# A float32 transformer block on one core: gate and up with another order of products, subtractions from PSUM, and down's low parts on GpSimd

## The chip, the cores and the metric

One core of a Trainium2 chip runs the whole program. Its engines are TensorE (PE in the profile; PEld are its weight loads), VectorE (DVE), ScalarE (ACT), GpSimd (POOL) and SyncE (SP), which here issues nearly all DMAs. The metric is the device time of one launch in microseconds (us), the median of several runs. "Faster" and "slower" are told against the kernel before.

## What is computed

The reference is one layer of a decoder with 512 tokens and model width 2048, all in float32: mixing (attention and convolution) with an output projection, then a feed-forward network. The change is in the second half:

```
h2 = _rms_norm(x, norm2_g)
x = x + (silu(h2 @ w_gate) * (h2 @ w_up)) @ w_down      # w_gate, w_up: 2048 x 5632, w_down: 5632 x 2048
```

The norm's factor is one number per token, so the kernel multiplies without it and puts it on the results: silu(r * gate) * (r * up).

## The kernel before

**Three products for one.** A float32 operand is split into a high part (the value rounded to the float32r format) and a low part (the rest), and each product is three matmuls: high x high, high x low, low x high (lines 1181, 1183, 1184 for gate and up; 1421 to 1423 for down). Each matmul here has 512 columns.

**Seven products for eight.** Gate, up and down each use Winograd's form of Strassen's scheme: 2 x 2 blocks take seven block products, numbered by `ORDER` (7, 1, 4, 2, 5, 6, 3) and, for down, `D_ORDER`, at the price of sums of blocks. The token side's sums are made once and stay in 56 slots as high and low halves (`ops`, seven products x eight pieces). The weights' sums are made while they stream in, by GpSimd (`plus`, line 172), in place in eight raw buffers.

**Steps.** I call half a product a step: one unit of weights (`next_unit`, line 292), two banks, twelve matmuls. Seven products are 14 steps, a half; a block (`Up(n)`, n = 0 to 10) is two halves, 28 steps, and makes 512 columns of gate and up. Down has 12 rounds (`Down(t)`) of 14 steps. Each step takes the sums due (`sums_now`), runs what is due in the list `evacs`, splits the weights that are two steps ahead (`split_up_to`: two ScalarE copies, `near` in PSUM at line 268 and `hi` at 269, and VectorE's low part at 270), asks for up to two loads (`pump`, line 234), issues its matmuls, and then runs what is due in the list `extras`. `later(n, ...)` puts a call n runs of its list ahead.

**The order of the work is written out by hand**: each engine's instructions run in the order in which the program issues them, so an instruction that waits holds up all behind it on its engine, and on SyncE a DMA that waits holds up all DMAs behind it.

**What follows a product** (`Up.done`, line 1197) is done in the step after its last. Four sums are kept per block, called (i, k): here i = 0 is gate and i = 1 up, k is the token half, and each lies in two tiles (a = 0, 1). A sum is complete after its last product of the second half. A bank is copied to a tile (`keep`, line 1191: ScalarE for a = 0, VectorE for a = 1) or added to it (`add`, line 1195). A product whose matmuls begin without `start` adds onto the one that lies in its banks: product 4 onto 7, 2 onto 1, 3 onto 5. Products 1 and 6 go to tiles of their own, and GpSimd then takes these from or adds them to the others (ten instructions a block, line 1195).

**What follows a block**: ScalarE's silu with the norm's factor (`gate`, line 1243), VectorE's product of the two with the factor (`weigh`, line 1252), VectorE's transposes of 32 x 32 blocks (`turn`, line 1256), a store to DRAM (`store`, line 1261). Steps are counted from 0: the weigh of token half 0 falls in step 1 of the next block, that of half 1 in step 2, the turns a step later. Then two pairs (`Pair`) are read back, from steps 6 and 16 of the next block on, as tiles l and r; GpSimd sums them (lines 1143 to 1148), and `piece` makes down's seven operands of each: a ScalarE copy `near` to PSUM (line 1110), a ScalarE copy for the high part (line 1114), VectorE's low part (line 1115), and a store (`od`, line 1100).

Beside it, sums for down's end are turned: `turn_x2` reads four pieces (z) and `turn_x2_now` transposes them on VectorE (zt, line 1288), at steps 9 and 12, 25 and 27 of blocks 1 to 8. `norm2` sums the squares on TensorE after step 2 of block 0.

All these tiles come from one pool of 73 slots (`slot`, line 138).

## Time and profile before

| what | value |
|---|---|
| median of 3 runs | 1947.52 us (1946.16 to 1948.61) |
| the profiled execution: its own time | 1949.01 us |
| its span, first to last instruction | 1947.3 us |
| mean granted TensorE clock | 0.984 |
| TensorE busy (modelled ends) | 1877.9 us |
| VectorE, ScalarE, GpSimd busy | 1480.2, 1365.2, 1085.8 us |
| gate and up, by their matmuls | 582 to 1506 us |
| down, by its matmuls | 1506 to 1943 us |

In the profile, a group's row has line, engine, operation, what it writes and reads (buffer numbers left out), shape and count, then busy us and mean ns, then the engine's idle time just before these instructions and what ended it. A window's row has the stretch in us from the span's start, its length, and for each engine the busy time with the number of instructions, then the granted clock, the share of the DMA engines and GB/s. Matmuls overlap and their ends are modelled, so a busy TensorE isn't one at its full pace: the distance between starts is what counts.

### The profile page before, as it was taken

What the parts mean: (1) busy time and instruction counts of PE and PEld (TensorE: products, weight loads), DVE (VectorE), ACT (ScalarE), POOL (GpSimd) and SP (SyncE); (2) the same over time, 40 slices, a digit from 0 to 9 for tenths busy, and PEclk for the clock granted to TensorE, in tenths of its full rate; (3) what the DMA queues carried; (4) which work ended last, traced back from release to release, by engine and by line L of the source; (5) the groups of instructions that cost most, each with busy time, mean ns of one, the idle gap of its engine ahead of it and who ended that gap; (6) DMA issues with size and microseconds to landing.
All of it is one profiled execution on the core that took longest, in us unless ns stands there. A gap on an engine that the chain in (4) does not pass through costs nothing.

```text
span 1947.3 us, 26413 instructions
## 1 busy us (share of the span) xinstructions
PE 1877.9 (96%) x8370; PEld 1542.3 (79%) x8370; DVE 1480.2 (76%) x2147; ACT 1365.2 (70%) x1893; POOL 1085.8 (56%) x762
## 2 busy tenths in 40 slices
PE   9999999999999998989989898998999799999999
PEld 7888888888887786877878687776878688888887
DVE  6788878997786767777776777777677777777777
ACT  6356544543567787878878787887879587777776
POOL 0135532100016566667566676756667588878776
PEclk9999999999999999999999999999999999999999
DMA  7242343244343376677657676666659897567545
GB/s 269 86 136 82 100 123 100 82 136 141 135 133 89 109 189 178 178 188 185 180 160 185 173 187 178 192 176 161 178 168 294 257 308 265 179 214 244 174 154 117
DMA packets 382987, 330.35 MB, mean 170 GB/s; under 512 B 171648, under 2 KB 311552, under 8 KB 382848
## 3 DMA queue, kind: packets, MB, share of 16 engines
q1 hardware_dynamic: 382704, 328.66, 57.5%
q8 instruction: 66, 1.08, 0.2%
q14 instruction: 73, 0.60, 0.1%
q10 hardware_dynamic: 144, 0.01, 0.0%
HBM read 255.56 MB, written 64.63 MB: 164 GB/s over the span
## 4 chain that ended last, share of the span: by engine, by line
PE 79%; DVE 7%; DMA 4%; SPq 3%; ACT 2%; POOL 2%; issue 2%; DVEq 0%; POOLq 0%; ACTq 0%
PE out L1183 10%; PE out L1184 10%; PE out L1181 10%; PE out L1422 7%; PE out L1421 7%; PE out L1423 7%; PE o L305 3%; PE o L303 3%; PE o L304 3%; DVE wl L270 2%; PE cq L303 2%; PE cq L305 1%; PE cq L304 1%; SPq L1130 1%; ACT wh L269 1%
## 5 line engine op out<-in xcount | busy, mean ns | idle before, releaser
L1183 PE MATMUL out<-wl,h 128*128 128x512 f32 x1232 | 491.9, 399 | 40.0 <-DVE wl L270 39.6
L1181 PE MATMUL out<-wh,h 128*128 128x512 f32 x1232 | 488.9, 397 | 10.6 <-DVE b8c L1195 1.7
L1184 PE MATMUL out<-wh,h 128*128 128x512 f32 x1232 | 488.1, 396 | 0.0
L1183 PEld LDWEIGHTS out<-wl,h 128*128 128x128 f32 x1232 | 236.0, 192 | 100.7 <-DVE wl L270 51.5
L1181 PEld LDWEIGHTS out<-wh,h 128*128 128x128 f32 x1232 | 236.2, 192 | 66.4 <-issue 13.5
L1184 PEld LDWEIGHTS out<-wh,h 128*128 128x128 f32 x1232 | 236.4, 192 | 48.3
L1421 PE MATMUL out<-wh,a 128*128 128x512 f32 x620 | 243.0, 392 | 8.6 <-issue 5.2
L1422 PE MATMUL out<-wl,a 128*128 128x512 f32 x620 | 242.7, 392 | 1.8 <-DVE wl L270 1.8
L1423 PE MATMUL out<-wh,a 128*128 128x512 f32 x620 | 242.3, 391 | 0.0
L274 ACT CAST wh<-w 128x1024 fp32r<-128x1024 f32 (+2 forms) x94 | 96.8, 1031 | 152.4 <-PE o L304 64.8
L252 DVE TENSOR_TENSOR wl<-w,wh 128x1024 fp32r<-128x1024 f32 (+2 forms) x95 | 113.3, 1192 | 40.9 <-ACT wh L274 39.2
L1421 PEld LDWEIGHTS out<-wh,a 128*128 128x128 f32 x620 | 117.7, 190 | 33.5 <-issue 5.6
L1422 PEld LDWEIGHTS out<-wl,a 128*128 128x128 f32 x620 | 117.6, 190 | 27.2 <-DVE wl L270 3.0
L1423 PEld LDWEIGHTS out<-wh,a 128*128 128x128 f32 x620 | 117.5, 190 | 24.0
L1431 DVE TENSOR_TENSOR y<-y,out 128x512 f32<-128x512 f32 x164 | 105.9, 683 | 21.4 <-PE out L1423 19.8
L514 DVE SCALAR_TENSOR_TENSOR y<-bu,cst,y 128x511 f32<-128x511 f32 (+14 forms) x120 | 89.9, 750 | 0.7
L303 PE MATMUL o<-mh_c,wh 128*128 128x512 f32 x128 | 51.1, 399 | 0.0
L303 PE MATMUL cq<-hh,wh 128*128 128x512 f32 x128 | 50.6, 395 | 0.0
L305 PE MATMUL o<-mh_c,wl 128*128 128x512 f32 x128 | 50.0, 391 | 0.0
L304 PE MATMUL cq<-hl,wh 128*128 128x512 f32 x128 | 50.0, 390 | 0.0
L305 PE MATMUL cq<-hh,wl 128*128 128x512 f32 x128 | 50.0, 390 | 0.0
L304 PE MATMUL o<-ml_c,wh 128*128 128x512 f32 x128 | 50.0, 390 | 0.0
(2411 smaller groups left out, 4955.6 us busy)
## 6 DMA issues: line engine op xcount, KB each, us to landing
od<-a SPq DMA_DIRECT2D x154, 256.0 KB, 4.9
a<-od SPq DMA_DIRECT2D x154, 256.0 KB, 5.5
w<-in_wi SPq DMA_DIRECT2D x58, 512.0 KB, 3.3
w<-in_wo SPq DMA_DIRECT2D x32, 512.0 KB, 3.3
x<-in_xT SPq DMA_DIRECT2D x16, 256.0 KB, 6.9
xr<-in_xT SPq DMA_DIRECT2D x16, 256.0 KB, 3.6
x2d<-xr SPq DMA_DIRECT2D x16, 256.0 KB, 2.0
z<-x2d SPq DMA_DIRECT2D x64, 64.0 KB, 4.9
```

Source lines behind the costliest of these rows:

```text
L252: fn(*args)
L274: (nc.vector.tensor_copy if u == 0 else nc.scalar.copy)(hi[:, :n], t[:, :n])
L303: nc.tensor.matmul(out, wh, xh, start=start, stop=False)
L304: nc.tensor.matmul(out, wh, xl, start=False, stop=False)
L305: nc.tensor.matmul(out, wl, xh, start=False, stop=stop)
L1181: nc.tensor.matmul(b, x[:, high], wh[:, s], start=c == f == 0 and q in (7, 1, 5, 6), stop=False, skip_group_check=True)
L1183: nc.tensor.matmul(b, x[:, high], wl[:, s], start=False, stop=False, skip_group_check=True)
L1184: nc.tensor.matmul(b, x[:, low], wh[:, s], start=False, stop=c == f == 1, skip_group_check=True)
L1421: nc.tensor.matmul(b[:, lo:hi], x[:, high], wh[:, s], start=start, stop=False, skip_group_check=True)
L1422: nc.tensor.matmul(b[:, lo:hi], x[:, high], wl[:, s], start=False, stop=False, skip_group_check=True)
L1423: nc.tensor.matmul(b[:, lo:hi], x[:, low], wh[:, s], start=False, stop=last, skip_group_check=True)
L1431: getattr(eng, op)(t, t, src)
```

## The change

Gate and up take their products in the order 7, 1, 4, 6, 5, 2, 3. Product 6 now lies on 1 in its banks, and their sum is read from PSUM three times: kept or added for (0, 1), and taken from both gate sums by VectorE (`less`). GpSimd's ten instructions a block go. Up and gate change places (through the weights' addresses: i = 0 is up now, i = 1 gate). From block 1 on the norm's factor is put on up's sums where they are read from the bank (`scale` in `keep` and `add`); block 0, whose factor isn't there in time, scales in `weigh`. The product of the two is made by GpSimd. `piece` loses its copy to PSUM: GpSimd subtracts the high part from the value, two steps later (`rest`). A pair is summed nine steps after its first read and not four; z is read at steps 9 and 23 and turned seven steps later. The loads of a step are asked for ahead of its split, so after the extras of the step whose split frees their buffers. The sums 21 + 22 and 21 + 11 of the weights are due two and four steps sooner, and the buffers rotate otherwise. `norm2` comes a step later.

```diff
-ORDER = (7, 1, 4, 2, 5, 6, 3)
+ORDER = (7, 1, 4, 6, 5, 2, 3)
...
-                                up_block(n // 2 * 2, int(k[0]) - 1, int(k[1]) - 1, n % 2 * 4 + 2 * i)))
+                                up_block(n // 2 * 2, 2 - int(k[0]), int(k[1]) - 1, n % 2 * 4 + 2 * i)))
...
-            sums[base + 2 + i].append(plus(key["21"], key["21"], key["22"], 1024))
-            sums[base + 6 + i].append(plus(key["11"], key["21"], key["11"], 1024))
-            sums[base + 7 + i].append(plus(key["12"], key["11"], key["12"], 1024))
+            sums[base + i].append(plus(key["21"], key["21"], key["22"], 1024))
+            sums[base + 2 + i].append(plus(key["11"], key["21"], key["11"], 1024))
+            sums[base + 7 + i].append(plus(key["11"], key["11"], key["12"], 1024))
         works.extend((keys[c][k], last, "moves") for k, last in (
-            ("s", True), ("11", False), ("22", True), ("12", False), ("21", True), ("11", True), ("12", True)) for c in "AB")
-        bufs = {c: {"21": b["22"], "11": b["21"], "s": b["11"], "22": b["s"]} for c, b in bufs.items()}
+            ("s", True), ("11", False), ("22", True), ("11", False), ("21", True), ("12", True), ("11", True)) for c in "AB")
+        bufs = {c: {"21": b["22"], "11": b["21"], "s": b["s"], "22": b["11"]} for c, b in bufs.items()}
...
+        moves = works[u][2] == "moves"
+        if moves:
+            pump(RAW_BUFS, 2)
         lows_now()
         split_up_to(u + SPLIT_AHEAD)
-        if not lows:
-            pump(RAW_EARLY if u < 20 else RAW_BUFS, 2 if works[u][2] == "moves" else 99)
+        if not lows and not moves:
+            pump(RAW_EARLY if u < 20 else RAW_BUFS)
...
-    def piece(name, p, at, src):
-        n = src.shape[-1] // TH
-        near = psum["high"].tile([P, 1024], F32R, name=f"{name}n{at}", tag="h")[:, :n * TH]
-        nc.scalar.copy(near, src)
-        for k in range(n):
-            q, s = LAID[at + k], slice(k * TH, (k + 1) * TH)
+    def piece(p, at, src):
+        for k in range(src.shape[-1] // TH):
+            q, part = LAID[at + k], by_turns(src[:, k * TH:(k + 1) * TH])
             t = slot(f"a{q}_{p}", F32R)
-            nc.scalar.copy(by_tiles(t[:, :TH]), by_turns(src[:, s]))
-            nc.vector.tensor_sub(by_tiles(t[:, TH:]), by_turns(src[:, s]), by_turns(near[:, s].bitcast(F32)))
-            later(0, nc.sync.dma_start, od[p][:, (at + k) * T:(at + k + 1) * T], t.bitcast(F32), queue=extras)
+            nc.scalar.copy(by_tiles(t[:, :TH]), part)
+            later(1, rest, p, at + k, t, part)
+
+    def rest(p, at, t, part):
+        nc.gpsimd.tensor_sub(by_tiles(t[:, TH:]), part, by_tiles(t[:, :TH].bitcast(F32)))
+        later(1, nc.sync.dma_start, od[p][:, at * T:(at + 1) * T], t.bitcast(F32), queue=extras)
...
-            for at, fn in ((0, self.read_l), (1, self.read_r), (4, self.sums), (5, self.piece_r), (7, self.piece_l),
-                           (8, self.sum4), (9, self.piece_a), (11, self.piece_4)):
+            for at, fn in ((0, self.read_l), (2, self.read_r), (9, self.sums), (10, self.piece_r), (12, self.piece_l),
+                           (13, self.sum4), (14, self.piece_a), (16, self.piece_4)):
...
-                        nc.tensor.matmul(b, x[:, high], wh[:, s], start=c == f == 0 and q in (7, 1, 5, 6), stop=False,
+                        nc.tensor.matmul(b, x[:, high], wh[:, s], start=c == f == 0 and q in (7, 1, 5, 2), stop=False,
...
         def keep(self, i, k, a, b):
             t = self.c[i, k, a] = slot(f"b{self.n}c{i}{k}{a}")
-            (nc.vector.tensor_copy if a else nc.scalar.copy)(t, b)
+            if a == 0:
+                nc.scalar.activation(t, b, AF.Copy, scale=1.0 if i or not self.n else self.scale(k, a))
+            elif i or not self.n:
+                nc.vector.tensor_copy(t, b)
+            else:
+                nc.vector.tensor_scalar(t, b, self.scale(k, a), None, op0=ALU.mult)

-        def add(self, i, k, a, src, eng=nc.vector, op="tensor_add"):
-            t = self.c[i, k, a]
-            getattr(eng, op)(t, t, src)
+        def add(self, i, k, a, b):
+            t = self.c[i, k, a]
+            if i or not self.n:
+                nc.vector.tensor_add(t, t, b)
+            else:
+                nc.vector.scalar_tensor_tensor(t, b, self.scale(k, a), t, op0=ALU.mult, op1=ALU.add)
+
+        def less(self, k, a, b):
+            t = self.c[1, k, a]
+            nc.vector.tensor_sub(t, t, b)
...
                 elif q == 1:
-                    self.keep(2, 0, a, b)
+                    by(0, 0, a, b)
                 elif q == 4:
                     by(1, 0, a, b)
-                elif q == 2:
-                    by(0, 0, a, b)
+                elif q == 6:
+                    by(0, 1, a, b)
+                    self.less(0, a, b)
+                    self.less(1, a, b)
                 elif q == 5:
-                    self.add(1, 1, a, b, op="tensor_sub")
-                elif q == 6:
-                    self.add(2, 0, a, b)
+                    self.less(1, a, b)
                 else:
-                    self.add(0, 1, a, b)
...
+            if first:
+                return
+            if q in (6, 5):
+                later(1, self.gate, 6 - q, queue=extras)
+            elif q == 2:
+                self.dram = tc.dram_tile([T, T], F32, name=f"bd{self.n}")
+            if q in (2, 3):
+                later(0, self.weigh, q - 2)
+                later(2, self.turn, q - 2)
+                later(3, self.store, q - 2, queue=extras)
+            if q == 3:
+                for at in range(2):
+                    later(5 + 13 * at, Pair, self.dram, 2 * self.n + at, at, queue=extras)
...
         def weigh(self, k):
             for a in range(2):
-                t = self.c[1, k, a]
-                nc.vector.scalar_tensor_tensor(t, t, self.scale(k, a), self.c[0, k, a], op0=ALU.mult, op1=ALU.mult)
+                t = self.c[0, k, a]
+                if not self.n:
+                    nc.vector.tensor_scalar(t, t, self.scale(k, a), None, op0=ALU.mult)
+                nc.gpsimd.tensor_mul(t, t, self.c[1, k, a])
...
-                    if n == 0 and at_unit == 2:
+                    if n == 0 and at_unit == 3:
                         norm2()
-                    if 1 <= n <= 8 and at_unit in (9, 12, 25, 27):
-                        (turn_x2 if at_unit % 16 == 9 else turn_x2_now)(SUMS[2 * n - 2 + at_unit // 16])
+                    if 1 <= n <= 8 and at_unit in (9, 23):
+                        key = SUMS[2 * n - 2 + at_unit // 16]
+                        turn_x2(key)
+                        later(6, turn_x2_now, key)
```

More of the change, by code (lines that the diff above doesn't have):

```diff
@@ L1216, in done @@
-            if q == 6:
-                u = [self.c.pop((2, 0, a)) for a in range(2)]
-                for a in range(2):
-                    self.add(1, 0, a, u[a], nc.gpsimd, "tensor_sub")
-                for a in range(2):
-                    if first:
-                        self.c[0, 1, a] = u[a]
-                    else:
-                        self.add(0, 1, a, u[a], nc.gpsimd)
-                for a in range(2):
-                    self.add(1, 1, a, u[a], nc.gpsimd, "tensor_sub")
@@ L1227, in done @@
-            if not first and q in (2, 3):
-                k = q - 2
-                if k == 0:
-                    self.dram = tc.dram_tile([T, T], F32, name=f"bd{self.n}")
-                later(0, self.gate, k, queue=extras)
-                at = 1 if k else 6
-                later(at, self.weigh, k)
-                later(at + 1, self.turn, k)
-                later(at + 2, self.store, k, queue=extras)
-            if not first and q == 3:
-                later(5, Pair, self.dram, 2 * self.n, 0, queue=extras)
-                later(15, Pair, self.dram, 2 * self.n + 1, 1, queue=extras)
@@ L1240, in gate @@
-        def gate(self, k):
-            for a in range(2):
-                g = self.c[0, k, a]
-                nc.scalar.activation(g, g, AF.Silu, scale=self.scale(k, a))
+                    self.less(1, a, b)
+                else:
+                    self.add(0, q - 2, a, b)
+            if first:
[4 more added lines that the diff above has]
+                self.dram = tc.dram_tile([T, T], F32, name=f"bd{self.n}")
@@ L1247, in scale, with gate @@
             return n2["r"][:, i:i + 1]
+        def gate(self, k):
+            for a in range(2):
+                t = self.c[1, k, a]
+                nc.scalar.activation(t, t, AF.Silu, scale=self.scale(k, a))
         def weigh(self, k):
             for a in range(2):
-                t = self.c[1, k, a]
-                nc.vector.scalar_tensor_tensor(t, t, self.scale(k, a), self.c[0, k, a], op0=ALU.mult, op1=ALU.mult)
+                t = self.c[0, k, a]
+                if not self.n:
+                    nc.vector.tensor_scalar(t, t, self.scale(k, a), None, op0=ALU.mult)
+                nc.gpsimd.tensor_mul(t, t, self.c[1, k, a])
         def turn(self, k):
             for a in range(2):
-                nc.vector.transpose(self.c[0, k, a], self.c.pop((1, k, a)))
+                nc.vector.transpose(self.c[1, k, a], self.c.pop((0, k, a)))
         def store(self, k):
```

10 lines of the change are left out of this document (5 added, 5 removed).

## The prediction, made before the changed kernel was run

> **What bounds the kernel now.** I read the page first (its group rows are quoted where used), then the windows by stage, by block, and of one block's first steps.
>
> ```profile
> 804.94:817.86 12.92, 12.92 (x58) 1.00 0.47 104
> ...
> core 0: us, PE busy (x) PEld busy (x) DVE busy (x) ACT busy (x) POOL busy (x), PEclk, DMA share, GB/s
> 582.00:1506.00 924.00, 871.20 (x3703) 706.05 (x3702) 675.77 (x812) 737.96 (x942) 613.44 (x363) 0.97 0.65 176
> ...
> 663.00:742.00 79.00, 77.51 (x338) 1.00 0.62 164
> 827.00:911.50 84.50, 79.34 (x339) 0.98 0.70 184
> 911.50:997.00 85.50, 80.00 (x338) 0.96 0.66 179
> ...
> 1253.62:1275.43 21.81, 15.08 (x63) 11.31 (x62) 17.90 (x20) 14.13 (x18) 12.89 (x8) 1.00 0.51 146
> 1275.43:1338.83 63.40, 63.14 (x277) 51.40 (x275) 44.49 (x57) 53.46 (x71) 43.89 (x27) 1.00 0.72 189
> ```
>
> TensorE is the bound (busy 871 of 924 us in gate and up, more than any other engine); what a change can win is the time between its matmuls. Each row has the stretch, its length and, for each engine, busy time and instructions (the rows with one such pair are TensorE's alone). The first of them is a stretch without a wait: 57 intervals in 12.92 us, 0.2267 us a matmul. Twelve make one of my steps (half a product), 2.72 us; 28 steps make a block, 76.2 us. By that pace the 3703 matmuls of gate and up need 839.5 of 924.0 us: **84.5 us are lost**. Block 1 loses 79.0 - 338 x 0.2267 = 2.4, block 3 7.7, block 4 8.9. The last two rows cut block 8 behind its fifth step: the loss is all in the first five (63 matmuls need 14.3 of 21.8 us); the other 23 run clean (277 need 62.8 of 63.4).
>
> What fills VectorE there (its groups in block 8's first steps, but zt's of the whole run; then both engines' instructions in order of time):
>
> ```profile
> L1252 DVE SCALAR_TENSOR_TENSOR b7c<-b7c,n2r,b7c 128x512 f32<-128x512 f32 x4 | 6.5, 1658 | 0.0
> L1256 DVE STREAM_TRANSPOSE b7c<-b7c 128x512 f32<-128x512 f32 x4 | 2.6, 680 | 0.0
> L1288 DVE STREAM_TRANSPOSE zt<-z 128x512 f32<-128x512 f32 x16 | 11.3, 708 | 32.2 <-DMA z<-x2d 12.0 <-DMA w('12', 'u18A')_12598<-in_wgu 4.4 <-DMA w('12', 'u6A')_8068<-in_wgu 4.2
> L1115 DVE TENSOR_TENSOR a<-p13r,p13n 128x256 fp32r<-128x256 f32 x1 | 0.4, 382 | 0.0
> ...
> 1261.95 5.12 DVE L1252 SCALAR_TENSOR_TENSOR b7c<-b7c,n2r,b7c 128x512 f32<-128x512 f32 x2
> 1266.99 1.21 DVE L270 TENSOR_TENSOR wl<-w('11', 'u16B')_11690,wn 128x1024 fp32r<-128x1024 f32 x1
> ...
> 1261.36 2.38 POOL L172 TENSOR_TENSOR w('21', 'u16B')_11588<-w('21', 'u16B')_11588,w('22', 'u16B')_11801 128x1024 f32<-128x1024 f32 x1
> 1263.70 2.81 POOL L172 TENSOR_TENSOR w('11', 'u16A')_11663<-w('21', 'u16A')_11559,w('11', 'u16A')_11663 128x1024 f32<-128x1024 f32 x1
> ...
> L1183 PE MATMUL out<-wl,h 128*128 128x512 f32 x1232 | 491.9, 399 | 40.0 <-DVE wl L270 39.6
> ```
>
> VectorE is busy 17.9 us and idle 3.9, the whole 21.8 where five steps give 13.6; the idle time is before zt, whose read hasn't landed (32.2 us over the run). Two weigh instructions (L1252) take 5.1 us together while GpSimd adds weights; the weights' low part (L270) stands behind them, and TensorE's largest wait is for that (last row). So two things make the loss: the weigh that drags beside GpSimd, and the transpose queued before its read is there.
>
> **The change part by part.** Rows for the prices:
>
> ```profile
> L1195 DVE TENSOR_TENSOR b7c<-b7c,out x18: 673/680/690, 1203.0 to 1260.2; 128x512 f32<-128x512 f32 x18
> L1195 POOL TENSOR_TENSOR b7c<-b7c,b7c x10: 1280/1290/1302, 1211.8 to 1257.8; 128x512 f32<-128x512 f32 x10
> L1252 DVE SCALAR_TENSOR_TENSOR b7c<-b7c,n2r,b7c x4: 703/1538/2853, 1261.9 to 1270.0; 128x512 f32<-128x512 f32 x4
> L648 DVE SCALAR_TENSOR_TENSOR ak2k<-ak2raw,gqk,ak2t x1: 747/747/747, 235.6 to 235.6; 128x512 f32<-128x512 f32 x1
> 235.04 0.82 POOL L781 TENSOR_SCALAR_AFFINE_SELECT c7pl<-c7lp 128x256 fp32r<-128x256 f32 x1
> L1143 POOL TENSOR_TENSOR p1a<-p1l x1: 737/737/737, 718.1 to 718.1; 128x256 f32<-128x256 f32 x1
> 800.48 1.01 ACT L268 CAST wn<-w('12', 'u5B')_7702 128x1024 fp32r<-128x1024 f32 x1
> L1110 ACT CAST p13n<-p13r x2: 374/483/592, 1236.3 to 1254.4; 128x512 fp32r<-128x512 f32 x1, 128x256 fp32r<-128x256 f32 x1
> L512 DVE TENSOR_SCALAR y<-bu,cst x4: 530/535/1511, 61.1 to 344.2; 128x512 f32<-128x512 f32 x4
> ```
>
> *VectorE, a block.* Gone: four weighs (6.5 us in block 8) and 14 low parts of down's operands (L1115, 14 x 0.4 = 5.6). New: 32 instructions that read a bank (14 in the first half, 18 in the second) for 23 (18 adds and 5 copies): 9 x 0.68 = 6.1. Fourteen of them take the norm's column as a pointer: L648 is that form (tensor, pointer, bank) and takes 0.747 beside a GpSimd instruction; 14 x 0.07 = 1.0. Net -5.0. In the first five steps: 17.9 - 6.5 - 0.4 + 4 x 0.07 = **11.3 of 13.6 us**, and zt's wait goes, since its transpose now stands seven steps behind the read (19 us) and not two. VectorE no longer sets the pace there.
>
> The Trainium skill, "SBUF — State Buffer", section "Who interferes with whom", says that a VectorE instruction with two SBUF inputs contends with a GpSimd one that reads SBUF, and one with at most one does not: L1252 (two) at 2.85 and L1195 (one, the other a bank) at 0.69 agree. Its "Perfetto Trace Analysis", "Optimizing Scalar/DVE Operations", warns that moving work between these two engines might not help as they share a port; by it the moved work would give back what it frees, which is the pointer rival below.
>
> *Product 6's evacuation*, three bank reads for each half, is six instructions in a row in the second half: 0.4 (the matmuls' end) + 2 x 0.75 + 4 x 0.68 + 1.2 for the next low part = 5.8 us in two steps of 5.44: 0.4 us late, once a block. The first half has five and fits.
>
> *ScalarE.* Gone: 8 near copies a block (two pairs of 3 x 0.59 + 0.37: 4.3 us), one of five bank copies. Nothing is late for it: 67.6 us a block become about 63. The PSUM buffers that the near copies took from the weights' split are free too.
>
> *GpSimd.* Gone: 10 subtractions and additions x 1.29 = 12.9. New: 4 weighs x 1.29 = 5.2 and 14 low parts of 256 columns. That form with reordered columns isn't in the trace on GpSimd: bounds 0.65 (half of the GpSimd L1195's 1.29) and 1.29; I take 0.74, L1143's, the same width: 10.4. Sum +2.7 a block, on 57 of 76. What counts is the order at a block's start: sum 21 A (2.4), the second pair's sums (3 x 0.74), 21 B (2.4), weigh (2.6), 11 A and 11 B (4.8): 14.4 us, 11 B's being needed when its split may start, 13.6 us in, and in truth before 15.7 (a split is two ScalarE copies of 1.0, L268's row, and L270's 1.2; its product is at 19.0). About one us of slack; the second weigh is through at 9.6, and VectorE, which transposes it in step 3 (from 8.2), can wait 1.4 us: its low part then lands at 12.3, needed at 13.6. I charge 0.2 a block.
>
> *The 22 reads.* The sum 21 + 22 is asked for two steps sooner while its read goes out a step later (behind the extras of the step, where the queue waited for the split anyhow).
>
> ```profile
> 1250.29 1.25 SPq L242 DMA_DIRECT2D w('22', 'u16B')_11801<-in_wgu  x2
> DMA to landing us min/median/max: 2.7/4.6/9.1
> od<-a SPq DMA_DIRECT2D x154, 256.0 KB, 4.9
> L1191 ACT COPY b9c<-out 128x512 f32<-128x512 f32 x5 | 2.9, 581 | 0.2 <-DMA bd<-b8c 0.2
> ```
>
> Block 8's 22 B is issued at 1250.3 to 1251.5 (first row; block 8 begins at 1253.6) and by the median of the weights' line (second row, L242) lands 2.5 us into the block, sum 21 B's turn being at 4.6: nothing. By the maximum it lands at 7.0: 2.4 us late. I take nothing and keep 2.4.
>
> *Down*, by the same pace, then its largest ScalarE wait:
>
> ```profile
> 1506.00:1522.00 16.00, 11.95 (x52) 9.23 (x50) 15.26 (x12) 10.86 (x15) 16.00 (x9) 1.00 0.80 298
> 1522.00:1530.00 8.00, 5.07 (x12) 3.69 (x13) 7.09 (x10) 3.01 (x3) 2.98 (x3) 0.57 0.36 112
> 1550.00:1566.00 16.00, 12.64 (x44) 9.79 (x43) 8.44 (x12) 10.14 (x15) 11.09 (x9) 0.79 1.02 322
> ACT p20n L1110 <- DMA p20r<-bd: 7.2, 1, 7.2
> ```
>
> 16 - 52 x 0.2267 = 4.2 and 5.3 us go at its start (block 10's weighs again) and 6.0 near 1558, where ScalarE waits 7.2 us for a pair's read: 15.5. Both go: l and r are asked for nine and seven steps ahead of their first use and not four and three. I leave 2 for GpSimd, which takes 14 low parts beside down's own sums.
>
> *The rest.* norm2 moves a step; block 0's loss (about 5, VectorE still busy with the operands) stays. Block 0 weighs with four extra VectorE scalings, SBUF to SBUF, the form of L512 (0.53 alone, 1.51 beside GpSimd), two of them in block 1's first steps: its 2.4 stays.
>
> **Sum.** Lost now 84.5 + 15.5 = 100.0. Left: block 0 5.0, block 1 2.4, nine blocks x (0.4 + 0.2) = 5.4, down 2: 14.8. Saved 85.2. Against the profiled execution (1949.0 us, span 1947.3) that is 1863.8; it stands 1.5 above the median shown, so **1862 us**. With every loss gone 1848.
>
> **The rivals.**
> *GpSimd late.* 22 B lands at 9.1 us, or a low part costs 1.29: either puts sum 11 B 2 to 3 us behind the split, at each block's start and in down: 11 x 3 = 33 us, 1895. For: 1 us of slack, one long queue. Against: GpSimd has run ahead of its due steps till now. 0.18.
> *The pointer counts as an SBUF input.* Then 14 evacuations a block drag as L1252 does, 0.9 us each on its mean of 1.66: 13 us of VectorE a block, most in the second half, where product 6's six instructions pass two steps by 2.2, and the first steps get 14.0 of 13.6: 4 a block over ten blocks, 1862 + 40 = 1902. Against: L648's 0.747. 0.07.
> *Slots run out (slower).* Seven products x 8 operand tiles hold 56 of 73 slots. A pair's l and r are now held 7 and 6 steps longer (their low parts counted), a low-part tile 2, so a ScalarE cast may get a slot whose od store is still under way (4.9 us to land); the b9c row shows one such wait now, 0.2 us. ScalarE would then have 63 + 8w us for eight pieces a block with a wait of w: past today's 84.5 from w = 2.7. At 3.5 it is 91: 1947.5 + 10 x 6.5 = 2012. For: more tiles, no more slots. Against: the weighed product needs no second temporary (two slots free). 0.12.
> *It doesn't do what it says*: the first steps' loss stays, because the weigh on GpSimd delays the transposes as long as it dragged before; only zt's wait (32.2 over the run, of which some 9 on the path) and down go: 15.5 + 9 = 24.5, 1923. Against: 1.4 us of wait, not 6. 0.03.
>
> **How the numbers follow.** Forecast (1848 to 1876) 0.60, the rivals 0.18, 0.07, 0.12, 0.03. The first three hold 0.85, so the range runs from the time without a loss to just past the pointer's: 1848 to 1905. A change of 0.2% (3.9 us) is about what a measurement here can tell from none. Faster 0.88; slower 0.10, the slots; the same 0.02, slots with a wait near the balance of 2.7 us.
>
> **What would show it.** Right: gate and up at 842 to 866 us; the first five steps of blocks 2 to 10 within 14.5 us; VectorE's bank reads with a pointer at 0.75; GpSimd's low parts at 0.74 and no wait of TensorE for L270 above 1 us; clock 0.99 or more. Wrong: ScalarE idle before casts into a with a DMA od as releaser (slots); SCALAR_TENSOR_TENSOR from a bank at 1.5 or more (pointer); the split waiting for L172 (GpSimd late).

## The result and the profile after

The changed kernel takes 1874.38 us (median of 4 runs, 1873.66 to 1878.16) where the kernel before takes 1946.84 in the same comparison (1945.66 to 1948.61): a ratio of 0.9631, 95% interval 0.9614 to 0.9648, 3.7% faster. The forecast was 1862, so 72 of the forecast 85 us came. The profiled execution took 1873.66 us, with a span of 1871.9 and a granted clock of 0.996.

First the windows of the changed kernel, in the order of columns that the prediction explains: gate and up, then block 8's first five steps and its other 23.

```profile
582.00:1428.00 846.00, 841.72 (x3707) 696.30 (x3706) 643.09 (x739) 699.51 (x850) 617.36 (x426) 1.00 0.69 191
1199.49:1213.09 13.60, 13.60 (x61) 11.26 (x60) 10.83 (x13) 11.98 (x16) 13.44 (x11) 1.00 0.59 193
1213.09:1275.65 62.56, 62.56 (x277) 51.80 (x276) 47.21 (x53) 51.72 (x62) 45.31 (x33) 1.00 0.78 201
```

Block 8 now takes 76.16 us, which is 336 x 0.2267: not one wait is left in it. Its first five steps take 13.6 us where they took 21.8, and VectorE has 10.8 us of work there, not 17.9. GpSimd is busy 13.44 of the 13.60 us, and nobody waits for it.

The groups of TensorE's matmuls on the page, with the idle time before them at the end of each row: gate and up's first two kinds and down's first.

```profile
L1184 PE MATMUL out<-wh,h 128*128 128x512 f32 x1232 | 480.5, 390 | 4.3 <-ACT wh L269 4.3
L1186 PE MATMUL out<-wl,h 128*128 128x512 f32 x1232 | 480.4, 390 | 0.0
...
L1431 PE MATMUL out<-wh,a 128*128 128x512 f32 x620 | 242.9, 392 | 11.5 <-ACT wh L269 11.5
```

The 39.6 us of waiting for VectorE's low part (L270) are 0.0. A single wait of 4.3 us is left in gate and up, in block 0, and down waits 11.5 us for ScalarE's high part (8.6 us of idle time before, of which 3.4 were for that part).

From here on I measure both stages in one way: from the start of the first matmul to that of the last, less the matmuls between at 0.2267 (3695 of them, 837.7 us, in gate and up; 1859, 421.4, in down). **Gate and up**: 924.4 before, 845.7 after, lost 86.7 and 8.0. **Down**: 435.5 before, 438.4 after, lost 14.1 and 17.0. So the whole gain is in gate and up. They lose 5 us less than forecast, and down, which was to lose 2, loses 15 more: that makes the 10 us by which the profiled execution is longer than the forecast for it (1863.8).

Lost time isn't all waiting. After some waits the granted clock is 0.5 for 3.4 or 6.8 us, and there the matmuls start 0.43 us apart. The row is such a stretch in the kernel before, just behind a wait of 3.1 us:

```profile
926.80:931.90 5.10, 5.10 (x13) 3.96 (x12) 5.10 (x8) 3.44 (x5) 0.00 (x0) 0.50 0.04 9
```

Before the change, 88 intervals in gate and up are of this kind, and they make 17.6 of the 86.7 us; after it 9, which make 1.8 of the 8.0. So a wait can cost more than its own length. What sets such a stretch off I haven't settled.

The prices that the prediction took, from the groups by shape (count, then minimum, median and maximum in ns):

```profile
L1206 DVE SCALAR_TENSOR_TENSOR b8c<-out,n2r,b8c x12: 744/750/751, 1231.0 to 1275.9; 128x512 f32<-128x512 f32 x12
...
L1118 POOL TENSOR_TENSOR a<-p2r,a x3: 737/743/750, 791.6 to 808.7; 128x256 fp32r<-128x256 f32 x3
...
L1259 POOL TENSOR_TENSOR b2c<-b2c,b2c x4: 1297/1310/1317, 813.0 to 825.0; 128x512 f32<-128x512 f32 x4
```

A bank read with the norm's pointer takes 0.75 and never drags, GpSimd's low part takes 0.74 and its weigh 1.31: as taken (0.75, 0.74 and 1.29).

**Where down loses.** TensorE waits for the split between 1468 and 1552, in down's rounds 1 to 3. The windows of down's first 72 us:

```profile
1428.00:1460.00 32.00, 31.85 (x139) 25.60 (x138) 24.62 (x29) 25.63 (x32) 29.41 (x23) 1.00 0.91 315
1460.00:1500.00 40.00, 32.38 (x126) 24.87 (x125) 17.84 (x21) 21.46 (x29) 27.03 (x21) 0.93 0.80 253
```

In the second of them every engine is idle for a good part, GpSimd too (27.0 of 40 us): nobody is short of time, something comes late. (The granted clock is 0.93 there, so a part of TensorE's loss is again slower matmuls.) ScalarE's split waits for GpSimd, and GpSimd for loads. The first view is ScalarE's list of waits, the second GpSimd in order of time.

```profile
ACT wn L268 <- POOL w('s', 'd1A')_14248 L172: 6.7, 1, 6.7
...
ACT wn L268 <- POOL w('21', 'd1A')_14068 L172: 5.3, 1, 5.3
```

```profile
1464.25 2.40 POOL L172 TENSOR_TENSOR w('s', 'd1A')_14248<-w('21', 'd1A')_14068,w('11', 'd1A')_14161 128x1024 f32<-128x1024 f32 x1 [4.10 <-DMA w('11', 'd1A')_14161<-in_wd]
...
1479.77 2.38 POOL L172 TENSOR_TENSOR w('21', 'd1A')_14068<-w('21', 'd1A')_14068,w('22', 'd1A')_14277 128x1024 f32<-128x1024 f32 x1 [6.28 <-DMA w('22', 'd1A')_14277<-in_wd]
```

And why the loads are late, in SyncE's issues (start, how long the issue took, what):

```profile
1449.33 3.70 SPq L1313 DMA_DIRECT2D y<-x2t  x4
1453.35 0.97 SPq L1103 DMA_DIRECT2D od<-a  x2
1454.65 3.26 SPq L1133 DMA_DIRECT2D p20l<-bd  x4
1458.36 1.70 SPq L242 DMA_DIRECT2D w('11', 'd1A')_14161<-in_wd  x1
...
1463.94 3.96 SPq L1133 DMA_DIRECT2D p20r<-bd  x4
1468.00 2.17 SPq L1103 DMA_DIRECT2D od<-a  x2
1470.27 2.09 SPq L1318 DMA_DIRECT2D a<-od  x4
1472.45 0.38 SPq L1103 DMA_DIRECT2D od<-a  x1
1472.93 0.38 SPq L242 DMA_DIRECT2D w('22', 'd1A')_14277<-in_wd  x1
```

SyncE issues without a pause from 1445 to 1476. The weights' loads (L242) stand in one queue behind the reads of pair 20 (3.3 and 4.0 us of issue for four DMAs), the y and a reads and the stores. With the change a pair is summed five steps behind its old place, the second one eight, so that the stores of pair 19 and all the work on pairs 20 and 21 fall deeper into down.

### The profile page after: what moved, and what is told of

Read it like the earlier page. It is cut to its first block, busy times and chain, and to the rows that moved or that the text cites. A ratio compares the mean times of both kernels' runs of the same rounds, so it can differ in the third digit from the quotient of the medians.

```text
span 1871.9 us, 26621 instructions
## 1 busy us (share of the span) xinstructions
PE 1849.2 (99%) x8370; PEld 1530.4 (82%) x8370; DVE 1432.8 (77%) x2052; ACT 1321.8 (71%) x1794; POOL 1106.1 (59%) x850
## 4 chain that ended last, share of the span: by engine, by line
PE 93%; POOL 2%; DMA 2%; issue 1%; DVE 1%; ACT 1%; SPq 0%; POOLq 0%; ACTq 0%; DVEq 0%
PE out L1184 15%; PE out L1186 15%; PE out L1187 15%; PE out L1431 6%; PE out L1432 6%; PE out L1433 6%; PE o L306 3%; PE o L308 3%; PE o L307 3%; PE cq L306 2%; PE cq L307 2%; PE cq L308 2%; PE ak L306 1%; PE aq L306 1%; PE av L306 1%
## 5 line engine op out<-in xcount | busy, mean ns | idle before, releaser
L1184 PE MATMUL out<-wh,h 128*128 128x512 f32 x1232 | 480.5, 390 | 4.3 <-ACT wh L269 4.3
L1186 PE MATMUL out<-wl,h 128*128 128x512 f32 x1232 | 480.4, 390 | 0.0
L1187 PE MATMUL out<-wh,h 128*128 128x512 f32 x1232 | 480.2, 390 | 0.0
L1184 PEld LDWEIGHTS out<-wh,h 128*128 128x128 f32 x1232 | 231.8, 188 | 52.8 <-ACT wh L269 4.7
L1186 PEld LDWEIGHTS out<-wl,h 128*128 128x128 f32 x1232 | 231.8, 188 | 48.4 <-DVE wl L270 0.3
L1187 PEld LDWEIGHTS out<-wh,h 128*128 128x128 f32 x1232 | 231.8, 188 | 48.3
L1431 PE MATMUL out<-wh,a 128*128 128x512 f32 x620 | 242.9, 392 | 11.5 <-ACT wh L269 11.5
```

The source lines that it names most:

```text
L1184: nc.tensor.matmul(b, x[:, high], wh[:, s], start=c == f == 0 and q in (7, 1, 5, 2), stop=False, skip_group_check=True)
L1186: nc.tensor.matmul(b, x[:, high], wl[:, s], start=False, stop=False, skip_group_check=True)
L1187: nc.tensor.matmul(b, x[:, low], wh[:, s], start=False, stop=c == f == 1, skip_group_check=True)
L1431: nc.tensor.matmul(b[:, lo:hi], x[:, high], wh[:, s], start=start, stop=False, skip_group_check=True)
```

## The experiments

| kernel | median us | ratio to before, 95% interval | gate and up | down |
|---|---|---|---|---|
| before (in the run of the change) | 1946.84 | | 924.4 | 435.5 |
| after | 1874.38 | 0.9631, 0.9614 to 0.9648 | 845.7 | 438.4 |
| e1: before, weigh off VectorE | 1911.86 | 0.9818, 0.9797 to 0.9838 | 889.8 | 433.1 |
| e2: before, z's new times | 1968.52 | 1.0102, 1.0087 to 1.0117 | 945.5 | 435.0 |
| e3: before, both | 1918.32 | 0.9843, 0.9828 to 0.9857 | 896.6 | 432.5 |
| e4: after, weigh on VectorE | 1881.52 | 0.9658, 0.9642 to 0.9674 | 855.5 | 435.3 |
| e5: e3 and the pairs' new times | 1890.06 | 0.9708, 0.9693 to 0.9722 | 857.7 | 443.1 |
| e6: after, all low parts on VectorE | 1928.58 | 0.9904, 0.9889 to 0.9919 | 893.1 | 443.7 |
| e7: after, low parts of pairs 20, 21 on VectorE | 1875.76 | 0.9638, 0.9624 to 0.9652 | 845.6 | 440.4 |
| e8: after, one load a step in round 0 | 1866.51 | 0.9585, 0.9569 to 0.9601 | 846.2 | 431.2 |
| e9: e8, last pairs later, block 0's sum later | 1857.99 | 0.9537, 0.9521 to 0.9553 | 843.6 | 423.2 |
| e10: after, the pairs' old times | 1873.12 | 0.9614, 0.9600 to 0.9628 | 858.0 | 425.4 |
| e11: after, loads behind the split | 1872.06 | 0.9608, 0.9593 to 0.9622 | 845.3 | 435.9 |
| e12: after, z's old times | 1872.01 | 0.9613, 0.9597 to 0.9629 | 845.1 | 438.4 |

Each ratio is against the kernel before as it ran beside that kernel. The stages are from each kernel's profiled execution. Two questions were open: what made gate and up faster, and what made down lose 17 us.

### e1: the kernel before with its weigh off VectorE

```diff
-nc.vector.scalar_tensor_tensor(t, t, self.scale(k, a), self.c[0, k, a], op0=ALU.mult, op1=ALU.mult)
+nc.scalar.activation(t, t, AF.Copy, scale=self.scale(k, a))
+nc.gpsimd.tensor_mul(t, t, self.c[0, k, a])
```

> The kernel before, with one edit: the weigh leaves VectorE (ScalarE puts the factor on, GpSimd multiplies). Theory 1 (the weigh that drags beside GpSimd makes most of the gate and up loss): of 84.5 us some 7 stay in blocks 0 and 1 and some 9 to zt's late reads, and about 9 more go at down's start, so 60 to 75 us go: 1872 to 1887 us, and blocks 2 to 10 lose under 2 us each in their first five steps. Rival A (zt's transposes behind late reads make most of it, 32.2 us of VectorE idle): under 30 us go, over 1917. Rival B (the gain needs the order of products that rids GpSimd of ten subtractions a block; with the multiply added GpSimd has 57 + 5 of 76 us and is late for the weights' sums): 1930 or more, with the split waiting for L172.

36 us went, between theory and rival. By steps (the intervals between matmuls that are at least 0.1 us longer than 0.2267, less 0.2267, summed over the blocks) theory 1 is right about its place: steps 3 and 4 lost 37.0 and 16.0 us before and lose 5.7 and 2.7 now. But step 2, which loses 27.9 us before, still loses 31.0; it was to go too. Its two waits a block are for the bank that VectorE reads late and for the low part behind it. Of the first five steps of block 8 this window tells:

```profile
1232.34:1250.09 17.75, 15.57 (x61) 12.24 (x60) 11.04 (x15) 14.64 (x20) 14.63 (x11) 0.90 0.66 179
```

VectorE has only 11.0 of 17.75 us to do, and yet TensorE waits: what is left is VectorE standing still, not VectorE at work.

### e2: the kernel before with z's new times

```diff
-                    if 1 <= n <= 8 and at_unit in (9, 12, 25, 27):
-                        (turn_x2 if at_unit % 16 == 9 else turn_x2_now)(SUMS[2 * n - 2 + at_unit // 16])
+                    if 1 <= n <= 8 and at_unit in (9, 23):
+                        key = SUMS[2 * n - 2 + at_unit // 16]
+                        turn_x2(key)
+                        later(6, turn_x2_now, key)
```

> The kernel before, with one edit: z is read at steps 9 and 23 and turned seven steps behind. Theory 1: only what of zt's 32.2 us of waiting lay on the path goes, some 9 us: about 1938 (1930 to 1943), VectorE's idle before zt falls to 0 and blocks 3 to 9 still lose 6 us and more each. Rival A: 30 us or more go, 1917 or less.

Slower by 1.0%: neither theory had that. Step 2's loss is gone, as it should be, and the first five steps together lose 58 us where they lost 81, though step 4 now loses 48.6. What makes the kernel slower is steps 25 and 26: 43.0 us where they lost 3.9. The next run has the same loss, and what it is made of is told there. VectorE in order of time at block 7's start:

```profile
1187.04 4.09 DVE L1252 SCALAR_TENSOR_TENSOR b6c<-b6c,n2r,b6c 128x512 f32<-128x512 f32 x2
...
1193.41 0.66 DVE L1288 STREAM_TRANSPOSE zt<-z 128x512 f32<-128x512 f32 x1
1194.00 2.96 DVE L1252 SCALAR_TENSOR_TENSOR b6c<-b6c,n2r,b6c 128x512 f32<-128x512 f32 x2
```

The second transpose now falls between the two weighs, in the first steps of the next block, where VectorE is short.

### e3: both

> The kernel before with both edits (weigh off VectorE, z read earlier). Theory 1: both losses go and block 0's 5 and block 1's 2.4 us stay with down's 6 near 1558: 1863 to 1872, at or under the changed kernel without its new order of products, PSUM subtractions, low parts on GpSimd or earlier loads. Rival B (these other parts carry the gain): over 1900.

1918, not 1863 to 1872, and slower than e1. The first five steps of blocks 1 to 10 lose nearly nothing now (step 2 0.0), so theory 1 holds for the place that it spoke of. But steps 25 and 26 lose 47.1 us where they lost 9.9 in e1. So z's new times bring this loss, here as in e2. First the waits of TensorE and of ScalarE, summed; then block 3's chain in order: GpSimd, SyncE, ScalarE:

```profile
PE out L1181 <- ACT wh L269: 29.4, 16, 3.3
...
ACT a L1114 <- DMA od<-a: 21.8, 8, 3.3
```

```profile
888.15 0.74 POOL L1144 TENSOR_TENSOR p5l<-p5l,p5r 128x256 f32<-128x256 f32 x1 [5.81 <-DMA p5r<-bd]
...
892.04 2.40 POOL L172 TENSOR_TENSOR w('11', 'u7B')_8306<-w('21', 'u7B')_8209,w('11', 'u7B')_8306 128x1024 f32<-128x1024 f32 x1
```

```profile
894.47 0.88 SPq L242 DMA_DIRECT2D w('11', 'u8B')_8682<-in_wgu  x2
895.47 0.87 SPq L1100 DMA_DIRECT2D od<-a  x2
```

```profile
900.35 0.41 ACT L1114 CAST a<-p5l 128x256 fp32r<-128x256 f32 x1 [3.04 <-DMA od<-a]
900.66 1.01 ACT L268 CAST wn<-w('12', 'u7A')_8444 128x1024 fp32r<-128x1024 f32 x1
```

GpSimd stands 5.8 us before a pair's sum whose read is late, and its weights' sums behind it end at 894.4. SyncE's next load has waited 6.1 us for the last of them, and the od stores stand behind this load: the first goes out at 895.47 and lands at 900.27. ScalarE stands 3.0 us before the cast of a down operand until this store has landed, and the split of the next weights, for which TensorE waits, stands behind the cast. The last wait is the one that the prediction's rival "slots run out" describes: a new tile gets a slot whose store is still under way. Step 25's loss (12.2 us) stands behind GpSimd's late sum alone, step 26's (34.9) behind the cast.

The same chain is in each of blocks 1 to 8 of e2 and of e3, with a wait of the cast of 2.5 to 3.3 us (21.8 in either run). These are the blocks in which z is read. Without the last link GpSimd's wait costs nothing there: it is as long in the kernel before (6.0 us for p5r) and in e1 (5.5), where the casts wait 0.4 us for an od store in the whole run, and in block 9 of e3 (5.6 for p17r), where steps 25 and 26 lose nothing. So what is new isn't that a first loss has gone, for e2 still has it; it is that a cast now needs this slot. The edit holds z's tiles for seven steps, not for three or two. That they take the slots is argued from the edit, as the trace names only the store.

### e5: e3 with the pairs' new times

The pair's list of times and the second pair's offset (15 to 18) are the changed kernel's.

> The kernel before with three edits: weigh off VectorE, z read earlier, and the pairs' times of the changed kernel (read at steps 6 and 19, summed nine steps behind their first read and not four). Theory 3, formed on the run with two edits: there blocks 1 to 8 lose 5 to 9 us each in steps 25 and 26, because GpSimd waits 5.8 us, in order, for a pair's read and is late with the weights' sums of the next half; without that wait the 47 us of those steps go: 1918 - 47 = 1871, 1868 to 1880, and GpSimd's idle time before p-sums with a DMA p r as releaser falls from 5.8 us a block to under 1. Rival (the sums are late because GpSimd has too much to do, ten subtractions and the multiply: the new order is needed): 1905 or more.

Steps 25 and 26 lose nothing, and gate and up are at 857.7: theory 3 is right on this, though it left out the links through SyncE and the slot. GpSimd's wait, the first link, is gone, and ScalarE's for an od store with it. In all it is 1890 and not 1871, because steps 4, 5 and 21 still lose 3.9, 7.5 and 4.3, and because down got longer by 10.6 us, 432.5 to 443.1. Ahead of step 21 ScalarE again waits for a store, now that of a zt:

```profile
ACT a L1114 <- DMA x2t<-zt: 25.3, 8, 4.1
```

With e10 (below), the longer down is the first sign that the pairs' times are what costs down.

So these three edits make 58 of the changed kernel's 72 us on the old order of products (the weigh isn't quite the changed kernel's: here ScalarE puts the factor on). Whether z's edit is needed among them wasn't run. The last 12 us of gate and up (857.7 to 845.7) come with the rest: the new order with ten GpSimd subtractions fewer, the low parts without near copies, the loads' place.

### e4, e10, e11 and e12: the changed kernel with one part taken back

e4 replaces `nc.gpsimd.tensor_mul` in `weigh` by `nc.vector.tensor_mul`:

> The changed kernel with its weigh back on VectorE (a product of two tiles in SBUF, no factor, same place in the order). Theory 1: it drags beside GpSimd, 0.7 alone and up to 2.9; in a block's first five steps VectorE has 11.3 + 2 x 1.66 to 2 x 2.85 = 14.6 to 17.0 of 13.6 us, so 1 to 3.4 us a block come back, over ten blocks 10 to 34: 1884 to 1908. Rival (the new order and the near copies that went make the room, wherever the weigh is): within 4 us of 1874.

Gate and up give back 9.8 us (855.5), just under the forecast 10 to 34; the total is 1881.5, just under the range, as down gained 3. But it isn't the 1 to 3.4 us a block of theory 1: more than half falls in block 1 (5.1 us in its first five steps), and blocks 3 to 8 lose next to nothing. The weigh does drag (up to 2.9 us beside GpSimd). Only half 1's falls in the first steps now, since product 2 comes second to last, and there is room for it in most blocks.

e10, the pairs' old times:

> The changed kernel with the pairs' times of the kernel before (read at steps 6 and 16, r a step behind l, summed four steps behind the first read). Theory 3: GpSimd, in order, waits 5 to 6 us a block for a pair's read again, and with its sums asked for sooner here it has less room behind it: blocks 1 to 10 lose 3 to 9 us each, 1900 to 1945 in all. Rival (with the ten subtractions gone GpSimd has the time to wait): 1874 to 1880.

The total is the same, just under the rival's range, but it is the sum of two changes that neither expectation had. GpSimd does wait, 7.0 to 7.8 us in each of blocks 1 to 8 (first row is one of them), and that costs nothing, as the rival said. But gate and up lose 12.3 us elsewhere, 11.0 of them in step 18, where TensorE waits for the low part (last row) while VectorE waits for zt's slot, which a low part on GpSimd releases (middle row). And down, with its last pairs done sooner, gains 13.0.

```profile
POOL p7l L1147 <- DMA p7r<-bd: 7.8, 1, 7.8
```

```profile
DVE zt L1296 <- POOL a L1118: 37.4, 7, 5.5
```

```profile
PE out L1186 <- DVE wl L270: 8.7, 8, 1.2
```

e11, the loads behind the split:

> The changed kernel with each step's loads behind its split, as before the change: they may take the buffers that this split frees, so they are issued a step sooner and ahead of the step's other DMAs. Theory D2 (down loses by late loads of weights): down's loss falls from 16 to 8 to 12 us, gate and up stay: 1866 to 1871. Rival (a load that stands in SyncE's queue for its buffer holds up the reads and stores behind it): gate and up lose something again, a wait before a split or for a pair's read: over 1876. Neither: within 2 us of 1874.

Gate and up stay (845.3), down gains 2.5 of its 17.0: a small part of what theory D2 asked for. The total is within about 2 us of the changed kernel's. The loads' place explains neither the gain nor much of down's loss.

e12, z's old times:

> The changed kernel with z's times of the kernel before (read at steps 9 and 25, turned three and two steps later). Theory 1: a transpose whose read hasn't landed holds VectorE's queue, and at step 27 that is just ahead of a block's start, where the banks of product 3 wait to be read; with the weigh alone moved, blocks 2 to 9 lost 2.2 to 3.0 us each there (step 2). By that 8 x 2.2 to 3.0 = 18 to 24 us come back: 1892 to 1898. Rival (VectorE has room now, 11.3 of 13.6 us, and takes the wait without loss): 1874 to 1879.

Nothing came back. The idle time before zt, 32.2 us before the change, is only 5.2 with z's old times in the changed kernel:

```profile
L1296 DVE STREAM_TRANSPOSE zt<-z 128x512 f32<-128x512 f32 x16 | 11.3, 707 | 5.2 <-DMA z<-x2d 5.2
```

So z's move, which clears step 2 on the kernel before (e1 to e3), isn't needed in the changed one. Why its reads land in time there I haven't settled.

### e6 and e7: the low parts on VectorE

`rest` uses `nc.vector.tensor_sub` for all pairs (e6), or for pairs 20 and 21 alone (e7).

> The changed kernel with the low parts of down's operands on VectorE (value less high part, both in SBUF). Theory: with two SBUF inputs each takes 0.4 us alone and up to some 1.5 beside GpSimd; most lie in a block's middle, where VectorE has room, so gate and up give back 0 to 6 us; GpSimd is rid of 14 x 0.75 = 10.5 us in down's first rounds, and if down's 16 us are GpSimd's lateness 9 to 12 of them go: 1862 to 1872. Rival (down's loss comes from late loads): down keeps 13 us or more, 1872 to 1882.

54 us slower than the changed kernel, far outside what I expected. The same instruction, by pair (minimum, median, maximum in ns), then one of them and, from GpSimd's timeline, its neighbour:

```profile
L1118 DVE TENSOR_TENSOR a<-p5r,a x3: 408/1970/2564, 917.3 to 937.0; 128x256 fp32r<-128x256 f32 x3
```

```profile
1007.18 2.61 DVE L1118 TENSOR_TENSOR a<-p7l,a 128x256 fp32r<-128x256 f32 x1
```

```profile
1007.06 2.46 POOL L172 TENSOR_TENSOR w('11', 'u10A')_9327<-w('11', 'u10A')_9327,w('12', 'u10A')_9489 128x1024 f32<-128x1024 f32 x1 [2.47 <-ACT wn L268]
```

0.41 us alone, 2.6 beside a weights' sum. I had priced it at 1.5 and put it in the block's middle; most of the loss is in step 5 (36.8 us over the run) and 24 (7.1), where the pairs' pieces meet the sums.

> The changed kernel with the low parts of the last two pairs alone on VectorE: 14 x 0.75 us of GpSimd's work go from down's first rounds, gate and up stay as they are. Theory D1 (down's 16 us are GpSimd's: low parts between the weights' sums): 9 to 12 us go, 1862 to 1866, and ScalarE's waits for L172 there all but vanish. Theory D2 (SyncE issues the weights' loads late, behind reads of p, y and a: down's second round's loads are issued 1458 to 1475 and land up to 1482.5): the waits of TensorE before 1485 (6 us of 16) stay, and under 5 us go in all: 1869 to 1874.

1875.8, and TensorE's waits before 1485 are as they were (6.0 us, 5.8 in the changed kernel): theory D1 falls. It isn't a clean removal, since the low parts then drag on VectorE, but the first waits of down come before any low part of pair 20.

### e8 and e9: down's reads

e8:

```diff
-                    load_next(2 if self.t == 0 else 1, FEED)
+                    load_next(1, FEED)
```

> The changed kernel with one load of a stored operand a step in down's first round, not two: 14 DMAs of 256 KB fewer in its first 38 us on SyncE's queue and on the DMA engines. Theory D2 (late loads): the weights' loads of the second round are issued some 8 us sooner and 8 us or more of down's 16 go: 1862 to 1867. Theory D1 (GpSimd): within 2 us of 1874. A price it may have: operands or y that come late in the next rounds, TensorE or VectorE waiting for a DMA a or y.

1866.5; down 431.2, 7.2 us shorter. The load of 22 A of the second round is issued at 1468.4, not 1472.9, and TensorE and VectorE show no wait for an a or a y. Theory D2 holds for over 40% of the loss. The edit also takes 14 DMAs off the DMA engines, which are busy for 0.91 of the changed kernel's first 40 us of down. That full DMA engines rather than the queue make the loss is not what e10 shows: their share there is 1.03, and down loses 4.0 us. The load of 22 A lands 6.4 us behind its issue in e10, and 6.7 in the changed kernel; what differs is when it is issued.

e9 adds these two edits:

```diff
-                    later(5 + 13 * at, Pair, self.dram, 2 * self.n + at, at, queue=extras)
+                    later(5 + 13 * at + 28 * (at + 1) * (self.n == NBLOCKS - 1), Pair, self.dram, 2 * self.n + at, at, queue=extras)
...
-            sums[base + 2 + i].append(plus(key["11"], key["21"], key["11"], 1024))
+            sums[base + (2 if n else 4) + i].append(plus(key["11"], key["21"], key["11"], 1024))
```

> The changed kernel with one load a step in down's first round, the last block's two pairs read and worked 28 and 56 steps later (in rounds 2 to 6, not 0 to 3; what they make is wanted in round 10), and in block 0 the weights' sums 21 + 11 two steps later. Two stages, told apart in the trace. Down: if the pairs' eight reads on SyncE (2.8 to 4.2 us of issue for each four) and their 24 GpSimd instructions (0.74 each) hold up the weights' loads and sums, the 9.2 us that down still loses with one load a step fall to 3 to 5; if what is left is due to the weights' own sums and the y adds, they stay at 8 to 10. Block 0: the sum 21 + 11 at 586.9 runs beside VectorE's low part of an operand, 2.65 us there and 0.42 elsewhere; without it block 0 loses about 5, as before the change, not 8.1; rival (norm2's later place makes it): it stays at 8. In all 1858 to 1861 by the first of each, 1866 by the second.

1858.0, the best kernel here: 0.9537 of the time before. Down loses 1.8 us of 17.0, and the window that had 40 us for 126 matmuls has 178 in 40; no p read stands among SyncE's issues:

```profile
1458.00:1498.00 40.00, 40.00 (x178) 33.13 (x177) 27.88 (x32) 29.80 (x32) 35.39 (x22) 1.00 0.74 251
```

```profile
1455.47 1.67 SPq L1313 DMA_DIRECT2D y<-x2t  x2
1458.31 0.32 SPq L1103 DMA_DIRECT2D od<-a  x1
1459.00 0.38 SPq L242 DMA_DIRECT2D w('22', 'd1A')_14245<-in_wd  x1
1460.45 0.32 SPq L1313 DMA_DIRECT2D y<-x2t  x1
```

The load of 22 A goes out at 1459.0. Set beside each other, from SyncE's and GpSimd's timelines:

| kernel | 22 A of round 1 issued, us into down | GpSimd busy in down's first 72 us | down lost |
|---|---|---|---|
| e9 | 33.0 | 64.9 | 1.8 |
| e10 | 37.3 | 62.2 | 4.0 |
| e8 | 39.7 | 63.3 | 9.7 |
| e11 | 42.9 | 57.9 | 14.4 |
| after | 45.0 | 56.4 | 17.0 |
| e7 | 46.0 | 56.1 | 19.0 |
| e12 | 46.6 | 56.3 | 17.0 |

The later the load, the larger the loss (e12 alone is out of line, by 2 us), and the busiest GpSimd goes with the smallest: it has the time for its work if the loads are there. Part of the order is consequence, since a TensorE that waits also delays the next steps' issues. Reads and GpSimd work of the pairs were moved together, so e9 alone doesn't part these two.

Block 0 loses 6.0 and not 8.1 us, the way its first expectation had it, though not down to the 5 that it named. VectorE's low part of an operand beside GpSimd's sum in the changed kernel, and without it in e9:

```profile
586.93 2.65 DVE L1034 TENSOR_TENSOR h<-tb,h 128x256 fp32r<-128x256 f32 x1
```

```profile
586.90 2.39 POOL L172 TENSOR_TENSOR w('11', 'u0A')_5517<-w('21', 'u0A')_5464,w('11', 'u0A')_5517 128x1024 f32<-128x1024 f32 x1 [9.79 <-DVE wl L270]
```

```profile
587.08 0.42 DVE L1034 TENSOR_TENSOR h<-tb,h 128x256 fp32r<-128x256 f32 x1
```

## Why the prediction was right, and where it was wrong

The sum was to leave 14.8 us lost; 25.0 are.

- **VectorE, a block: right in size, incomplete as a cause.** 11.3 of 13.6 us were forecast for the first five steps, 10.8 came, and blocks 1 to 10 lose nothing. That the weigh and zt's read made these steps' loss is shown on the kernel before (e1, e3). That their removal is all it takes is refuted by e3: with z's new times a cast waits for a slot whose store GpSimd's late sum holds up, and steps 25 and 26 lose 47 us. The prediction didn't ask what z's move does to the slots. It held because the changed kernel is free of this: on the old order the pairs' times clear it (e5), and the changed kernel doesn't have it even with the pairs' old times (e10), where GpSimd waits 7 us and no cast waits for an od store. Why it has the slots there (the new order frees two) is argued, not shown.
- **Product 6's evacuation (0.4) and GpSimd at a block's start (0.2): too dear.** Nine blocks x 0.6 = 5.4 and block 1's 2.4 didn't come.
- **The 22 reads at nothing: right**; e11 takes the loads' place back and gate and up stay the same.
- **Block 0: 5.0 forecast, 8.0 measured.** "norm2 moves a step" was weighed there; the sum 21 + 11, due four steps sooner, was not, and it meets the operands' low parts on VectorE. e9 gives 2.1 us of it back.
- **Down: the step that failed.** "Both go ... I leave 2 for GpSimd, which takes 14 low parts beside down's own sums": the two old losses did go, and 17.0 us came. I priced the last pairs' later times by GpSimd's work (0.74 a low part), and not by what they put into SyncE's queue while down's first loads are to go out. e8, e9 and, from the other side, e5 and e10 (+10.6 and -13.0 us with the pairs' times) show it; e7 shows that the low parts don't make the first waits.
- **The rivals.** GpSimd late: it came in down alone (the split waits for L172), behind late loads; gate and up are free of it. The pointer: refuted, 0.75. Slots: no wait of ScalarE's casts for a store is among its larger waits in the changed kernel; the mechanism is real in e10, on VectorE, where it takes 11 us, and on the old order in e2 and e3 (21.8 us of ScalarE's waiting for an od store) and e5 (25.3 for zt's). The prediction counted the slots of the pairs and the low parts, and not those of z, which is now held four and five steps longer. It doesn't do what it says: refuted, 13.6 us.
- **The warning of the Trainium skill**, "Perfetto Trace Analysis", "Optimizing Scalar/DVE Operations", that moving work between VectorE and GpSimd might not help: here it did, by 36 us for the weigh (e1, where the factor goes to ScalarE too) and 54 for the low parts (e6 against the changed kernel).

What stays open: how the last 12 us of gate and up (e5 to the changed kernel) divide between the new order and the low parts without near copies; why the changed kernel has slots enough where e2 and e3 haven't; and how much of pairs 20 and 21's cost to down is their reads' and stores' place on SyncE, and how much their sums on GpSimd ahead of the weights'.

## What to carry to other kernels

When a read is moved ahead of its use, its tile is held longer, and another engine may then wait for a slot: here z's read, two steps sooner and turned seven steps behind, cleared one wait (28 us in step 2) and brought another (some 40 us in steps 25 and 26). And a wait that costs nothing (GpSimd's 6 us for a pair's read) begins to cost when somebody comes to need what stands behind it: before summing what a change removes, look for every in-order wait of over a step and follow it through the queues. A block that has the same wait and no loss, like block 9 of e3, tells which link is the new one. When a step is moved later, look at the end of the loop too: what used to end in the last block then runs into the next stage, with its DMAs in the same issue queue as that stage's first loads. And work whose result isn't wanted for a long time (the last pairs, eight rounds ahead) is best put where the queues are quiet.

## What the runs showed of the hardware

A VectorE instruction with two SBUF inputs doesn't slow down beside GpSimd; it stands until GpSimd's running instruction ends. In e6 GpSimd's sum runs from 1007.06 to 1009.52 and VectorE's low part, from 1007.18, ends at 1009.79, 0.27 behind it; in block 0 of the changed kernel the sum ends at 589.29 and the low part of an operand at 589.58, 0.29 behind. All 91 of e6's low parts that began beside a running GpSimd instruction end 0.28 to 0.31 us behind it. So the price is what is left of the GpSimd instruction, up to 2.4 us for a 0.41 us subtraction. The Trainium skill, "SBUF — State Buffer", "Who interferes with whom", calls the shared port pair an exclusive lock, and the traces agree. The other way round, GpSimd's low part with both inputs in SBUF takes 0.73 to 0.78 in every pair.

SyncE takes 3.3 to 4.0 us to issue the four reads of a pair's half when down's first loads crowd the queue, and mostly 0.4 us for a plain load of weights. In down's first 72 us the median is 0.95 us for a pair's DMA of 64 KB and 0.38 for a load of 512 KB, though single loads of weights took up to 1.70: a small read can hold the queue longer than a large one.
